# Gate and up products of both FFNs as seven half-size products instead of eight

## The chip, the cores and the metric

The kernel runs on one core of a Trainium2 chip. The metric is the device time of one execution in microseconds (us). Three runs of the kernel before gave a median of 1416.69 us (1415.98 to 1417.25). One further execution was taken by the hardware profiler.

The engines, by the names that the profile uses: PE is TensorE (matrix products, into PSUM), PEld its weight loads, DVE is VectorE, ACT is ScalarE, POOL is GpSimd, SP is SyncE, which here only issues DMAs (its queue is SPq). POOL issues DMAs too (POOLq).

## The reference

One layer for 512 tokens of width 1024 (`T = 512`, `D = 1024`, `FF = 2816`), all in float32:

```python
def swiglu(x, w_gate, w_up, w_down):
    return (jax.nn.silu(x @ w_gate) * (x @ w_up)) @ w_down

f = swiglu(rmsnorm(x, ffn1_pre_g[l]), ffn1_w_gate[l], ffn1_w_up[l], ffn1_w_down[l])
x = x + 0.5 * rmsnorm(f, ffn1_post_g[l])
y = hybrid_mixer(rmsnorm(x, mix_pre_g[l]), ...)   # windowed attention and mLSTM, merged
x = x + rmsnorm(y, mix_post_g[l])
f = swiglu(rmsnorm(x, ffn2_pre_g[l]), ffn2_w_gate[l], ffn2_w_up[l], ffn2_w_down[l])
x = x + 0.5 * rmsnorm(f, ffn2_post_g[l])
```

The change concerns `x @ w_gate` and `x @ w_up` in the two calls of `swiglu`. The mixer between them stays as it is.

## The kernel before, in words

Every float32 matrix product is made of three products of a rounded type (float32r): each operand is split into a high part and a low part, `ACT` casts the high part and `DVE` subtracts it from the original to get the low part, and PE accumulates high x high, high x low and low x high in one PSUM bank. `load_w` does this for a weight tile of 128 x 1024: SP issues a DMA into a buffer `wf` (three of them), ACT writes `wh`, DVE writes `wl` (five buffers each). The function `ws` then issues the products: for 8 blocks of 128 rows and 3 terms, 24 matmuls of 128x512.

The FFN (`ffn`) runs in two stages. In the first, the hidden width of 2816 is cut into `NF = 22` blocks of 128, the loop variable is `f`. For each block a gate tile and an up tile are loaded (`load_w`, L66 to L75), PE makes the two products (2 x 24 matmuls, L161) into two PSUM banks `pg`, ACT takes `silu` of the gate bank (tile `s`) and DVE multiplies it with the up bank into `aT[:, f, :]` (`close`, L224 and L225). The first two blocks (`EARLY = 2`) run interleaved in token halves (`by_halves`, L171, matmuls of 128x256), because the transposed input `hTh`/`hTl` (high and low part of the normalised tokens, [128, 8, 512] each) is still being finished. In the second stage (`down`) each `aT` block is split into `ah` and `al` (L246, L247), and PE accumulates 24 matmuls of 128x512 for each block into eight banks `acc` (L211 to L213). Names carry an `_a` for the first FFN and a `_b` for the second.

The program is written in Tile: the order of the instructions of each engine is set by a scheduler when the program is built, and buffers of one tag are handed on as their readers finish. Each engine works through its instructions strictly in that order, and one that waits holds up all that stand behind it. SP's queue in this stage holds nothing but weight loads; POOL's holds the vectors of gains, the small constants of the mixer and one `pow` for each normalisation.

Of the kernel before, what the change touches and what calls it, by code (L numbers as in the profile page):

```python
# [10 lines left out]
F32 = mybir.dt.float32  # L11
F32R = mybir.dt.float32r
# [4 lines left out]
P = 128  # L17
# [22 lines left out]
def tile_hybrid_block(ctx: ExitStack, tc: tile.TileContext, a: dict):  # L40
    nc = tc.nc

    const = ctx.enter_context(tc.tile_pool(name="const", bufs=1))
    wpool = ctx.enter_context(tc.tile_pool(name="wpool", bufs=1))
    act = ctx.enter_context(tc.tile_pool(name="act", bufs=1))
    small = ctx.enter_context(tc.tile_pool(name="small", bufs=4))
    psum = ctx.enter_context(tc.tile_pool(name="psum", bufs=8, space=bass.MemoryType.PSUM))
# [6 lines left out]

    warm = act.tile([P, 512], BF16, tag="tmp", bufs=1, name="warm")[:, 0:256]
# [4 lines left out]
    ident = const.tile([P, P], F32, name="ident")  # L60
    make_identity(nc, ident)
# [4 lines left out]
    def load_w(src, name, n=1024, after=()):  # L66
        wf = wpool.tile([P, WMAX], F32, tag="wf", bufs=3, name=f"wf_{name}")[:, :n]
        nc.sync.dma_start(wf, src)
        with ExitStack() as st:
            for i in after:  # L70
                st.enter_context(tc.issue_after(i))
            wh = wpool.tile([P, WMAX], F32R, tag="wh", bufs=5, name=f"wh_{name}")[:, :n]
            nc.scalar.copy(wh, wf)  # L73
            wl = wpool.tile([P, WMAX], F32R, tag="wl", bufs=5, name=f"wl_{name}")[:, :n]
            nc.vector.tensor_tensor(wl, wf, wh.bitcast(F32), op=ALU.subtract)  # L75
        return wh, wl

    def gain(src, name, eng=None):
        g = act.tile([P, D], F32, tag="gain", bufs=2, name=f"g_{name}")
        (eng or nc.gpsimd).dma_start(g, src.partition_broadcast(P))  # L80
        return g

    def rsqrt(v, n, name):
        r = small.tile([P, n], F32, tag="r", name=f"r_{name}")
        nc.gpsimd.tensor_tensor(r, v, nhalf[:, :n], op=ALU.pow)
        return r
# [90 lines left out]
    def new_hT(name):  # L177
        hTh = act.tile([P, KD, T], F32R, tag="hTh", name=f"hTh_{name}")
        hTl = act.tile([P, KD, T], F32R, tag="hTl", name=f"hTl_{name}")
        return hTh, hTl  # L180
# [36 lines left out]

    def ffn(pool, todo, first_w, hT, wgu, wd, post, finish, name, later=None, pins=()):
        hTh, hTl = hT
        aT = pool.tile([P, NF, T], F32, name=f"aT_{name}")  # L220

        def close(f, pg):
            s = pool.tile([P, T], F32, tag="s", bufs=2, name=f"s_{name}{f}")
            nc.scalar.activation(s, pg[0], AF.Silu)  # L224
            nc.vector.tensor_tensor(aT[:, f, :], pg[1], s, op=ALU.mult)  # L225
        early = []
        for f in range(EARLY):
            wg, wu = first_w if first_w and f == 0 else [load_w(wgu[f, b], f"{name}gu{f}{b}", after=pins if f + b else ()) for b in range(2)]
            early.append((wg, wu, pair(f"pg_{name}{f}")))
        by_halves([(pg, (wg, wu)) for wg, wu, pg in early], hTh, hTl, todo)  # L230
        for f in range(EARLY):
            close(f, early[f][2])
        if later:
            later()
        for f in range(EARLY, NF):
            wg = load_w(wgu[f, 0], f"{name}g{f}")
            wu = load_w(wgu[f, 1], f"{name}u{f}")
            pg = pair(f"pg_{name}{f}")
            ws(pg[0], wg, KD, hTh, hTl)
            ws(pg[1], wu, KD, hTh, hTl)  # L240
            close(f, pg)

        def get_x(kk):
            ah = pool.tile([P, T], F32R, tag="ah", bufs=5, name=f"ah_{name}{kk}")
            al = pool.tile([P, T], F32R, tag="al", bufs=5, name=f"al_{name}{kk}")
            nc.scalar.copy(ah, aT[:, kk, :])  # L246
            nc.vector.tensor_tensor(al, aT[:, kk, :], ah.bitcast(F32), op=ALU.subtract)  # L247
            return ah, al

        return down(pool, NF, lambda kk: wd[kk], get_x, post, finish, todo, name)  # L250


    with tc.tile_pool(name="ffn_a", bufs=1) as fa:
        hbuf = [(act, "h"), (fa, "h2")]
        tbuf = [(act, "tmp"), (fa, "tmp2")]
        def load_x(t):
# [10 lines left out]
        first_w = [load_w(a["wgu1"][0, b], f"agu0{b}", after=pins if b else ()) for b in range(2)]  # L267
        todo = []
# [21 lines left out]

        pins = ffn(fa, todo, first_w, hT1, a["wgu1"], a["wd1"], post1, finish1, "a", load_gains)
    hTh, hTl = hT


    mctx = ExitStack()
    mix = mctx.enter_context(tc.tile_pool(name="mix", bufs=1))
    atth = mix.tile([P, HEADS, T], F32R, name="atth")
    attl = mix.tile([P, HEADS, T], F32R, name="attl")
    cw = mix.tile([P, 16, 5], F32, name="cw")
    nc.gpsimd.dma_start(cw, a["convwb"])  # L300

# [3 lines left out]
    ropeS = ap_.tile([32, 1, T], F32, name="ropeS")  # L305
    nc.gpsimd.dma_start(ropeC, a["ropeC"])
    nc.gpsimd.dma_start(ropeS, a["ropeS"])
    masks = ap_.tile([P, 512], BF16, name="masks")
    nc.gpsimd.dma_start(masks, a["masks"])
# [4 lines left out]
    nc.gpsimd.dma_start(gb, a["gbias"])  # L314
    SWAP = [(i + 16) % 32 for i in range(32)]

    def qk_evac(h, g, pq):
        q = ap_.tile([P, 2, T], F32, tag="qk", bufs=4, name=f"qk_{h}{g}")
        for b in range(2):
            nc.scalar.copy(q[:, b, :], pq[b])  # L320
        for b in range(2):
            sw = act.tile([32, T], F32, tag="h", bufs=1, name=f"sw_{h}{g}{b}")
# [180 lines left out]

    ga = act.tile([4, 2, T], F32, tag="tmp", bufs=1, name="ga")
    gb4 = act.tile([4, 2, T], F32, tag="h", bufs=1, name="gb4")
    gc4 = act.tile([4, 2, T], F32, tag="gain", bufs=2, name="gc4")
# [3 lines left out]
    selr = act.tile([4, D], F32R, tag="gain", bufs=2, name="selr")  # L510
    Gh = selr[:, 512:1024]
# [32 lines left out]
    caus = mix.tile([P, 1, P], F32, name="caus")  # L544
    nc.gpsimd.dma_start(caus[:, 0, :], a["caus"])
    hg = act.tile([P, 1, D], F32, tag="gain", bufs=2, name="hg")
    nc.gpsimd.dma_start(hg[:, 0, :], a["mlstm_head_g"].partition_broadcast(P))
# [221 lines left out]

    g_post2 = gain(a["ffn2_post_g"], "f2post")  # L770
    with tc.tile_pool(name="ffn_b", bufs=1) as fb:
        def post3(t):
            return PostNorm(t, g_post2, [(act, "tmp"), (fb, "tmp2")][t % 2], "f2", True)
# [5 lines left out]
        ffn(fb, todo, None, hT2, a["wgu2"], a["wd2"], post3, finish3, "b", pins=pins)  # L779

# [30 lines left out]
def _layout(inp):  # L811
# [57 lines left out]
```

## Time and profile before

| | us |
|---|---|
| median of three runs | 1416.69 |
| the profiled execution | 1415.97 |
| its span in the trace | 1414.2 |
| PE busy (share of the span) | 1401.5 (99%) |
| DVE busy | 624.5 (44%) |
| ACT busy | 487.8 (34%) |
| first FFN, blocks 2 to 21 of gate and up, on the chain that ended last | 217.63 |
| second FFN, the same blocks | 217.63 |
| granted TensorE clock, mean | 0.999 |

A busy PE means that matmuls followed one another without a gap. Their ends are modelled and overlap the next one's start, so the pace is read from the distance of starts or from the length of a stretch divided by its count, not from the mean duration of one.

### The profile page before, as it was taken

What the parts mean: (1) busy time and instruction counts of PE and PEld (TensorE: products, weight loads), DVE (VectorE), ACT (ScalarE), POOL (GpSimd) and SP (SyncE); (2) the same over time, 40 slices, a digit from 0 to 9 for tenths busy, and PEclk for the clock granted to TensorE, in tenths of its full rate; (3) what the DMA queues carried; (4) which work ended last, traced back from release to release, by engine and by line L of the source; (5) the groups of instructions that cost most, each with busy time, mean ns of one, the idle gap of its engine ahead of it and who ended that gap; (6) DMA issues with size and microseconds to landing.
All of it is one profiled execution on the core that took longest, in us unless ns stands there. A gap on an engine that the chain in (4) does not pass through costs nothing.

```text
span 1414.2 us, 16603 instructions
## 1 busy us (share of the span) xinstructions
PE 1401.5 (99%) x6752; PEld 1185.0 (84%) x6752; DVE 624.5 (44%) x986; ACT 487.8 (34%) x761; POOL 29.1 (2%) x52
## 2 busy tenths in 40 slices
PE   8999999999999999999999999999999999999998
PEld 8888888888899889888888888888888888888886
DVE  5332222233772775565756743333374222222333
ACT  5322222232533632344544543222264222222222
POOL 1000000000110000000000000000010000000000
PEclk9999999999999999999999999999999999999999
DMA  6433333333143222222222232323323323333321
GB/s 238 119 92 102 96 98 95 99 90 92 50 123 110 86 75 75 77 73 75 83 82 77 86 106 75 104 90 92 102 75 119 103 92 96 98 102 92 90 75 60
DMA packets 37357, 133.12 MB, mean 94 GB/s; under 512 B 4268, under 2 KB 4268, under 8 KB 37280
## 3 DMA queue, kind: packets, MB, share of 16 engines
q1 hardware_dynamic: 36144, 128.50, 29.2%
q0 software_dynamic: 1136, 3.56, 0.9%
q8 instruction: 53, 0.87, 0.3%
q14 instruction: 24, 0.20, 0.0%
HBM read 129.95 MB, written 2.10 MB: 93 GB/s over the span
## 4 chain that ended last, share of the span: by engine, by line
PE 95%; DVE 2%; ACT 1%; issue 1%; DMA 0%; POOL 0%; SPq 0%; POOLq 0%; DVEq 0%; ACTq 0%
PE pg_b L161 15%; PE pg_a L161 15%; PE p L161 11%; PE pq L161 7%; PE pm L161 6%; PE acc_b L211 3%; PE acc_b L212 3%; PE acc_b L213 3%; PE acc_a L213 3%; PE acc_a L211 2%; PE acc_a L212 2%; PE pvo L591 2%; PE pvo L593 2%; PE pvo L592 2%; PE pg_a L171 2%; PE pg_b L171 2%
## 5 line engine op out<-in xcount | busy, mean ns | idle before, releaser
L211 PE MATMUL acc_a<-wh_ad,ah_a 128*128 128x512 f32 x176 | 69.5, 395 | 0.0
L211 PE MATMUL acc_b<-wh_bd,ah_b 128*128 128x512 f32 x176 | 69.4, 395 | 0.0
L213 PE MATMUL acc_b<-wl_bd,ah_b 128*128 128x512 f32 x176 | 69.4, 395 | 0.0
L212 PE MATMUL acc_b<-wh_bd,al_b 128*128 128x512 f32 x176 | 69.4, 395 | 0.0
L212 PE MATMUL acc_a<-wh_ad,al_a 128*128 128x512 f32 x176 | 69.4, 395 | 0.0
L213 PE MATMUL acc_a<-wl_ad,ah_a 128*128 128x512 f32 x176 | 69.4, 395 | 0.0
L161 PE MATMUL pq<-hTh_mx,wh_qk 128*128 128x512 f32 x160 | 63.5, 397 | 0.0
L161 PE MATMUL pq<-hTl_mx,wh_qk 128*128 128x512 f32 x160 | 62.4, 390 | 0.0
L161 PE MATMUL pg_b<-hTl_f,wh_bg 128*128 128x512 f32 x160 | 62.3, 389 | 0.0
L161 PE MATMUL pg_a<-hTl_f,wh_ag 128*128 128x512 f32 x160 | 62.3, 389 | 0.0
L161 PE MATMUL pg_a<-hTh_f,wh_ag 128*128 128x512 f32 x160 | 62.3, 389 | 0.0
L161 PE MATMUL pg_b<-hTh_f,wh_bg 128*128 128x512 f32 x160 | 62.3, 389 | 0.0
L161 PE MATMUL pg_a<-hTh_f,wh_au 128*128 128x512 f32 x160 | 62.2, 389 | 0.0
L161 PE MATMUL pg_a<-hTl_f,wh_au 128*128 128x512 f32 x160 | 62.2, 389 | 0.0
L161 PE MATMUL pg_b<-hTh_f,wh_bu 128*128 128x512 f32 x160 | 62.2, 389 | 0.0
L161 PE MATMUL pg_b<-hTl_f,wh_bu 128*128 128x512 f32 x160 | 62.2, 389 | 0.0
L75 DVE TENSOR_TENSOR wl_bd<-wf_bd,wh_bd 128x1024 fp32r<-128x1024 f32 x22 | 26.9, 1224 | 71.7 <-ACT wh_bd L73 71.7
L75 DVE TENSOR_TENSOR wl_ad<-wf_ad,wh_ad 128x1024 fp32r<-128x1024 f32 x22 | 26.9, 1224 | 71.8 <-ACT wh_ad L73 71.8
L75 DVE TENSOR_TENSOR wl_bu<-wf_bu,wh_bu 128x1024 fp32r<-128x1024 f32 x20 | 24.5, 1225 | 70.0 <-ACT wh_bu L73 62.3
L75 DVE TENSOR_TENSOR wl_au<-wf_au,wh_au 128x1024 fp32r<-128x1024 f32 x20 | 24.5, 1225 | 69.3 <-ACT wh_au L73 63.7
L73 ACT CAST wh_bd<-wf_bd 128x1024 fp32r<-128x1024 f32 x22 | 23.1, 1051 | 88.1 <-PE acc_b L212 70.2
L73 ACT CAST wh_ad<-wf_ad 128x1024 fp32r<-128x1024 f32 x22 | 23.1, 1051 | 88.0 <-PE acc_a L212 70.2
(339 smaller groups left out, 3419.4 us busy)
## 6 DMA issues: line engine op xcount, KB each, us to landing
wf_qk<-in_wqk SPq DMA_DIRECT2D x24, 512.0 KB, 3.6
wf_ad<-in_wd SPq DMA_DIRECT2D x22, 512.0 KB, 3.5
wf_bd<-in_wd SPq DMA_DIRECT2D x22, 512.0 KB, 3.5
wf_ag<-in_wgu SPq DMA_DIRECT2D x20, 512.0 KB, 3.6
wf_au<-in_wgu SPq DMA_DIRECT2D x20, 512.0 KB, 3.6
wf_bg<-in_wgu SPq DMA_DIRECT2D x20, 512.0 KB, 3.5
wf_bu<-in_wgu SPq DMA_DIRECT2D x20, 512.0 KB, 3.6
wf_mqk<-in_wmqk SPq DMA_DIRECT2D x16, 512.0 KB, 3.6
```

Source lines behind the costliest of these rows:

```text
L73: nc.scalar.copy(wh, wf)
L75: nc.vector.tensor_tensor(wl, wf, wh.bitcast(F32), op=ALU.subtract)
L161: nc.tensor.matmul(out, lhsT=wt[:, k * P:(k + 1) * P], rhs=x[:, k, tok], start=n == 0, stop=n == len(terms) - 1)
L171: nc.tensor.matmul(outs[b][:, tok], lhsT=ws_[b][w][:, k * P:(k + 1) * P], rhs=x[:, k, tok], start=i + k + hf == 0, stop=hf == 1 and i == 2 ...
L211: nc.tensor.matmul(out, lhsT=xh[:, tk], rhs=wh[:, cs], start=first, stop=False)
L212: nc.tensor.matmul(out, lhsT=xl[:, tk], rhs=wh[:, cs], start=False, stop=False)
L213: nc.tensor.matmul(out, lhsT=xh[:, tk], rhs=wl[:, cs], start=False, stop=last)
L591: nc.tensor.matmul(out, lhsT=hTh[:, k, tk], rhs=wh[:, cs], start=k == 0, stop=False)
L592: nc.tensor.matmul(out, lhsT=hTl[:, k, tk], rhs=wh[:, cs], start=False, stop=False)
L593: nc.tensor.matmul(out, lhsT=hTh[:, k, tk], rhs=wl[:, cs], start=False, stop=k == KD - 1)
```

## The change

For blocks `f` = 4 to 21 of both FFNs (`PLAIN = 4`; 18 blocks each), gate and up are no longer two products of [128 x 1024] by [1024 x 512]. They are written as one 2x2 block product: the contraction of 1024 is cut into two halves of 512, the tokens into two halves of 256, and gate and up are the two rows. Eight half-size products (128 x 512 by 512 x 256) are replaced by seven, each with 12 matmuls of 128x256 (L307), by a scheme of the Strassen kind. It needs sums of weight quarters, sums of input quarters and sums of results.

- Weights (`load_quads`): a block holds four quarters of 128 x 512, `q0` to `q3`. SP loads `f1` (q0 and q1), `f4` (q3) and `ab` (q2, twice); then POOL issues a DMA that adds q0 and q3 from memory onto the two halves of `ab` (`accum_op`, it waits until the load of `ab` has landed). DVE adds `f4` to the first half of `ab` into `cd[:, 0]` (L261) and `f1[:, 1]` to that into `cd[:, 1]` (L262). `f1`, `cd`, `ab` and `f4` are each split by ACT (L238) and DVE (L239) into the high and low parts for products 1 and 2, 6 and 3, 7 and 5, and 4. In the names below the number of the block and of the first product run together: `wl_a107` is block 10, product 7.
- Inputs (`token_parts`): four sums of input quarters, once for each FFN, made while blocks 2 and 3 run. The unused end of `aT` is the scratch.
- Results (`seven`): ACT copies product 1 out of PSUM (`q1`), DVE adds it to what the bank `qb` holds (`uv`, L331), and after further products makes `z` (L338, L339, L313); `silu` is taken in two halves, and DVE multiplies (L314). Product 4 of a block is issued inside the next block (`finish`).
- Memory: pools now stand on two sides of SBUF, scratch tiles that lived in `act` move to a pool `work` that is opened for each phase; `wf` moves to `act`. The loads of the gains for the post norms move from the first blocks to the start of `down` (`begin`). The mixer's small constants are issued behind the last `pow` of the first FFN (`mixer_from`).
- The host lays out gate and up of a block side by side ([22, 128, 2048] instead of [22, 2, 128, 1024]).

```diff
+    def load_quads(src, low, scr, name):
+        q = src.rearrange("p (q c) -> p q c", c=Q)
+        f1 = act.tile([P, 2, Q], F32, tag="wf", bufs=3, name=f"f1_{name}")
+        f4 = scr.tile([P, Q], F32, tag="wf4", bufs=2, name=f"f4_{name}")
+        ab = act.tile([P, 2, Q], F32, tag="wf", bufs=3, name=f"ab_{name}")
+        nc.sync.dma_start(ab, q[:, 2:3, :].broadcast_to([P, 2, Q]))
+        nc.sync.dma_start(f1, q[:, 0:2, :])
+        nc.sync.dma_start(f4, q[:, 3, :])
+        nc.gpsimd.dma_start(ab, q[:, 0:4:3, :], accum_op=ADD)
...
+        pair_of((1, 2), f1)
+        cd = scr.tile([P, 2, Q], F32, tag="cd", bufs=1, name=f"cd_{name}")
+        nc.vector.tensor_tensor(cd[:, 0, :], ab[:, 0, :], f4, op=ADD)
+        nc.vector.tensor_tensor(cd[:, 1, :], cd[:, 0, :], f1[:, 1, :], op=ADD)
+        pair_of((6, 3), cd)
+        pair_of((7, 5), ab)
...
+    def token_parts(low, tmp, hTh, hTl, name):
...
+        nc.vector.tensor_tensor(f[5], b11, b12, op=SUB)
+        nc.vector.scalar_tensor_tensor(f[6], f[5], -1.0, b22, op0=MUL, op1=SUB)
+        part(6)
+        part(5)
+        nc.vector.tensor_tensor(f[7], b22, b12, op=SUB)
+        part(7)
+        nc.vector.scalar_tensor_tensor(f[4], f[6], -1.0, b21, op0=MUL, op1=SUB)
+        part(4)
...
+    def seven(fs, wgu, x, low, scr, aT, name):
...
+        for f in fs:
...
+            product(a1, w[1], 1, True, False)
+            nc.scalar.copy(q1, a1)
+            product(b1, w[6], 6, True, False)
+            product(c1, w[5], 5, False, False)
+            nc.vector.tensor_tensor(uv, bc, q1[:, None, :].broadcast_to([P, 2, H]), op=ADD)
+            if prev:
+                finish(prev)
+            product(a1, w[2], 2, False, True)
+            nc.scalar.activation(s[:, 0, :], a1, AF.Silu)
+            product(b1, w[7], 7, False, False)
+            product(c1, w[3], 3, False, True)
+            nc.vector.tensor_tensor(z[:, 1, :], b1, uv[:, 1, :], op=ADD)
+            nc.vector.tensor_tensor(z[:, 2, :], c1, uv[:, 0, :], op=ADD)
+            nc.scalar.activation(s[:, 1, :], z[:, 2, :], AF.Silu)
...
-        for f in range(EARLY, NF):
-            wg = load_w(wgu[f, 0], f"{name}g{f}")
-            wu = load_w(wgu[f, 1], f"{name}u{f}")
-            pg = pair(f"pg_{name}{f}")
-            ws(pg[0], wg, KD, hTh, hTl)
-            ws(pg[1], wu, KD, hTh, hTl)
-            close(f, pg)
+            for f in range(EARLY, PLAIN):
...
+                    x = token_parts(low, aT[:, NF - 16:, :], hTh, hTl, name)
...
+            seven(range(PLAIN, NF), wgu, x, low, scr, aT, name)
```

What the scheduler makes of it is seen on DVE and on SP in the middle of the first FFN's gate and up stage. DVE before, for two blocks (`wl` is the low part of a gate tile `ag` or an up tile `au`, `aT_a` the product that closes a block):

```order
L75 TENSOR_TENSOR wl_ag9_901<-wf_ag9_897,wh_ag9_899 128x1024
L75 TENSOR_TENSOR wl_au9_907<-wf_au9_903,wh_au9_905 128x1024
L225 TENSOR_TENSOR aT_a_195<-pg_a7_1_780,s_a7_829 128x512
L75 TENSOR_TENSOR wl_ag10_966<-wf_ag10_962,wh_ag10_964 128x1024
L75 TENSOR_TENSOR wl_au10_972<-wf_au10_968,wh_au10_970 128x1024
L225 TENSOR_TENSOR aT_a_195<-pg_a8_1_845,s_a8_894 128x512
```

DVE in the changed kernel, for one block's worth of work (from one `cd` to the next there are these eleven; block 11's weights, block 10's `uv`, block 9's results):

```order
L261 TENSOR_TENSOR cd_a11_1473<-ab_a11_1464,f4_a11_1463 128x512
L239 TENSOR_TENSOR wl_a107_1357<-ab_a10_1340,wh_a107_1356 128x1024
L262 TENSOR_TENSOR cd_a11_1473<-cd_a11_1473,f1_a11_1462 128x512
L239 TENSOR_TENSOR wl_a111_1470<-f1_a11_1462,wh_a111_1469 128x1024
L338 TENSOR_TENSOR z_a9_1244<-qb_a9_1241,uv_a9_1243 128x256
L339 TENSOR_TENSOR z_a9_1244<-qb_a9_1241,uv_a9_1243 128x256
L239 TENSOR_TENSOR wl_a116_1477<-cd_a11_1473,wh_a116_1476 128x1024
L331 TENSOR_TENSOR uv_a10_1367<-qb_a10_1365,q1_a10_1366 128x512
L313 TENSOR_TENSOR z_a9_1244<-qb_a9_1241,q1_a9_1242 128x256
L239 TENSOR_TENSOR wl4_a11_1485<-f4_a11_1463,wh4_a11_1484 128x512
L314 SCALAR_TENSOR_TENSOR aT_a_205<-z_a9_1244,s_a9_1245 128x512
```

Three instructions of a block have become eleven, and the first of them, the sum of block 11 that needs the accumulated `ab_a11`, stands ahead of the split of block 10's `ab`.

SP's weight loads before, for three blocks:

```order
L68 DMA wf_ag9_897<-in_wgu1 128x1024
L68 DMA wf_au9_903<-in_wgu1 128x1024
L68 DMA wf_ag10_962<-in_wgu1 128x1024
L68 DMA wf_au10_968<-in_wgu1 128x1024
L68 DMA wf_ag11_1027<-in_wgu1 128x1024
L68 DMA wf_au11_1033<-in_wgu1 128x1024
```

SP's weight loads in the changed kernel, for two blocks (`ab` is the load of the doubled quarter onto which POOL's DMA then adds):

```order
L248 DMA f4_a11_1463<-in_wgu1 128x512
L246 DMA ab_a11_1464<-in_wgu1 128x2x512
L247 DMA f1_a11_1462<-in_wgu1 128x1024
L248 DMA f4_a12_1587<-in_wgu1 128x512
L246 DMA ab_a12_1588<-in_wgu1 128x2x512
L247 DMA f1_a12_1586<-in_wgu1 128x1024
```

Two loads of a block have become three, with a fourth on POOL's queue. In the built program the `f1` of every block lies in the same one of the three buffers of tag `wf`, and `ab` alternates between the other two, so the load of `ab_a12` overwrites `ab_a10` and waits for the last reader of it, `wl_a107`.

More of the change, by code (lines that the diff above doesn't have):

```diff
@@ L78, in gain @@
     def gain(src, name, eng=None):
-        g = act.tile([P, D], F32, tag="gain", bufs=2, name=f"g_{name}")
+        g = work.tile([P, D], F32, tag="gain", bufs=2, name=f"g_{name}")
         (eng or nc.gpsimd).dma_start(g, src.partition_broadcast(P))
         return g
+    last_pow = [None]
     def rsqrt(v, n, name):
         r = small.tile([P, n], F32, tag="r", name=f"r_{name}")
-        nc.gpsimd.tensor_tensor(r, v, nhalf[:, :n], op=ALU.pow)
+        last_pow[0] = nc.gpsimd.tensor_tensor(r, v, nhalf[:, :n], op=ALU.pow).ins
         return r
@@ L219, in ffn @@
+    PLAIN = 4
+    def ffn(pool, todo, first_w, hT, wgu, wd, post, finish, name, begin=None, pins=()):
         hTh, hTl = hT
         aT = pool.tile([P, NF, T], F32, name=f"aT_{name}")
[L222 to L229, printed above, removed]
@@ L248, in get_x @@
             return ah, al
[L250 to L255, printed above, removed]
+        pins = down(pool, NF, lambda kk: wd[kk], get_x, post, finish, todo, name)
+        dn.close()
+        return pins
+    with new_pool("ffn_a") as fa:
+        hbuf = [(work, "h"), (work, "h2")]
+        tbuf = [(work, "tmp"), (work, "tmp2")]
+        op_ctx = ExitStack()
+        work.pool = op_ctx.enter_context(new_pool("opening"))
         def load_x(t):
@@ L266, in tile_hybrid_block @@
             turned = pins[0]
-        first_w = [load_w(a["wgu1"][0, b], f"agu0{b}", after=pins if b else ()) for b in range(2)]
+        first_w = [load_w(a["wgu1"][0, :, b * 1024:(b + 1) * 1024], f"agu0{b}", after=pins if b else ()) for b in range(2)]
         todo = []
@@ L305, in tile_hybrid_block @@
     ropeS = ap_.tile([32, 1, T], F32, name="ropeS")
[L306 removed]
+    with tc.issue_after(mixer_from):
+        nc.gpsimd.dma_start(ropeC, a["ropeC"])
     nc.gpsimd.dma_start(ropeS, a["ropeS"])
     masks = ap_.tile([P, 512], BF16, name="masks")
[L309 removed]
+    with tc.issue_after(mixer_from):
+        nc.gpsimd.dma_start(masks, a["masks"])
     perm = ap_.tile([P, 72], F32, name="perm")
@@ L313, in tile_hybrid_block @@
     gb = mix.tile([4, 2], F32, name="gb")
-    nc.gpsimd.dma_start(gb, a["gbias"])
+    with tc.issue_after(mixer_from):
+        nc.gpsimd.dma_start(gb, a["gbias"])
     SWAP = [(i + 16) % 32 for i in range(32)]
@@ L509, in tile_hybrid_block @@
     ones4, Gm = gc4[:, 0, :], gc4[:, 1, :]
-    selr = act.tile([4, D], F32R, tag="gain", bufs=2, name="selr")
+    selr = work.tile([4, D], F32R, tag="gain", bufs=2, name="selr")
     Gh = selr[:, 512:1024]
@@ L544, in tile_hybrid_block @@
     caus = mix.tile([P, 1, P], F32, name="caus")
-    nc.gpsimd.dma_start(caus[:, 0, :], a["caus"])
-    hg = act.tile([P, 1, D], F32, tag="gain", bufs=2, name="hg")
+    with tc.issue_after(mixer_from):
+        nc.gpsimd.dma_start(caus[:, 0, :], a["caus"])
+    hg = work.tile([P, 1, D], F32, tag="gain", bufs=2, name="hg")
     nc.gpsimd.dma_start(hg[:, 0, :], a["mlstm_head_g"].partition_broadcast(P))
@@ L767, in tile_hybrid_block @@
     mctx.close()
-    g_post2 = gain(a["ffn2_post_g"], "f2post")
-    with tc.tile_pool(name="ffn_b", bufs=1) as fb:
+    g_post2 = []
+    with new_pool("ffn_b") as fb:
         def post3(t):
-            return PostNorm(t, g_post2, [(act, "tmp"), (fb, "tmp2")][t % 2], "f2", True)
+            return PostNorm(t, g_post2[0], [(work, "tmp"), (work, "tmp2")][t % 2], "f2", True)
         def finish3(t):
```

160 lines of the change are left out of this document (128 added, 32 removed).

## The prediction

> **What bounds the kernel now.** I read the page's busy shares and slices first, then the chain that ended last, then the stretch of gate and up, then single durations.
>
> ```profile
> span 1414.2 us, 16603 instructions
> PE 1401.5 (99%) x6752; PEld 1185.0 (84%) x6752; DVE 624.5 (44%) x986; ACT 487.8 (34%) x761; POOL 29.1 (2%) x52
> PEclk9999999999999999999999999999999999999999
> DMA  6433333333143222222222232323323323333321
> PE 95%; DVE 2%; ACT 1%; issue 1%; DMA 0%; POOL 0%; SPq 0%; POOLq 0%; DVEq 0%; ACTq 0%
> ```
>
> PE has work 99% of the span at full clock, and the chain is PE for 95% of it. No other engine and no transfer sets the time; only less work on PE, or a new wait, can change it. The chain in order of time (start, length, what) gives PE's pace:
>
> ```profile
> 21.90 15.35 PE pg_a L171 x128
> 37.24 217.63 PE pg_a L161 x960
> ...
> 1067.48 217.63 PE pg_b L161 x960
> ```
>
> 128 matmuls of 256 columns take 15.35 us, 0.120 each; 960 of 512 columns take 217.63 us, 0.2267 each. A block of gate and up (48 matmuls) is 217.63 / 20 = 10.88 us. The same stretch by windows (PE, PEld, DVE, ACT, POOL busy, then clock, DMA share, GB/s):
>
> ```profile
> 37.20:254.90 217.70, 217.70 (x962) 180.31 (x961) 63.68 (x65) 56.67 (x64) 0.00 (x0) 1.00 0.33 100
> ```
>
> DVE is busy 29% here, ACT 26%, the DMA engines 33%. There is room beside PE, and the change fills it.
>
> **PE's part.** A changed block has 7 x 12 = 84 matmuls of 256 columns: 84 x 0.120 = 10.07 us for 10.88. That is 0.81 us, or 7.4%, not the eighth that seven for eight promises, because a matmul of half the width takes 53% of the time. The wider rows of the list of groups say the same if read rightly: their mean is a latency (283 ns against 389), and the starts are what count.
>
> ```profile
> L171 PEld LDWEIGHTS pg_a<-hTh_f,wh_agu x64: 186/192/192, 11.9 to 33.0; 128*128 128x128 f32 x64
> ```
>
> A weight load shows 192 ns, which would make 16.1 us of 84; but in that stretch a load went with every matmul and the pace was 0.120, so the loads overlap. If nothing else waits, 2 FFNs x 18 blocks x 0.81 = 29 us go.
>
> **DVE and ACT.** Durations by shape:
>
> ```profile
> L75 DVE TENSOR_TENSOR wl_ag<-wf_ag,wh_ag 128x1024 fp32r<-128x1024 f32 x20 | 24.3, 1215 | 0.0
> L225 DVE TENSOR_TENSOR aT_a<-pg_a,s_a 128x512 f32<-128x512 f32 x22 | 15.2, 691 | 85.3 <-PE pg_a L161 84.6 <-ACT s_a L224 0.8
> L601 DVE TENSOR_TENSOR vml<-pvo,vmh 128x256 fp32r<-128x256 f32 x16 | 6.7, 420 | 0.0
> L73 ACT CAST wh_ag<-wf_ag 128x1024 fp32r<-128x1024 f32 x20 | 21.1, 1054 | 50.9 <-PE pg_a L161 50.9
> L246 ACT CAST ah_a<-aT_a 128x512 fp32r<-128x512 f32 x22 | 13.6, 618 | 6.5 <-DVE aT_a L225 6.5
> L603 ACT ACTIVATE so<-pvo 128x256 f32<-128x256 f32 x16 | 6.2, 385 | 12.5 <-DVE vml L601 12.5
> L247 DVE TENSOR_TENSOR al_a<-aT_a,ah_a 128x512 fp32r<-128x512 f32 x22 | 15.1, 684 | 0.0
> ```
>
> DVE's eleven instructions of a block: three splits of 1024 columns (3 x 1.22), five of 512 columns (two sums `cd`, the split `wl4`, `uv`, the closing product, 5 x 0.69) and three `z` of 256 (3 x 0.42): 8.4 us. ACT: 3 x 1.05 + 0.62 + three of 256 columns at 0.385 = 4.9 us. Both are below 10.07, so neither is the bound by its sum, but DVE is full enough that the order of its instructions matters. `token_parts` is four sums, four combinations and four splits of 1024 columns, 12 x 1.22 = 14.6 us of DVE once for each FFN, beside blocks 2 and 3 (21.8 us of PE), where DVE has only 2 x 3.1 us of its own: it just fits. SP issues three loads instead of two, POOL one more; POOL has nothing else there. All of these lie beside PE and I cost them at nothing; if `token_parts` overran, it would cost its overrun once.
>
> **The ring, on which the forecast rests.** In the changed order DVE's sum `cd_a11` waits for the accumulating DMA of block 11, and queued behind it on DVE are `wl_a107` (PE's products 5 and 7 of block 10 need it), the first split of block 11 and the `z` of block 9 (product 4 of block 9 needs its first). So PE runs at most about one block ahead of the accumulates. And the accumulates feed themselves: `ab_a12` may be loaded only after `wl_a107` has read `ab_a10`; `wl_a107` stands behind `cd_a11`; `cd_a11` waits for accumulate 11; accumulate 12 waits for the load of `ab_a12`. One turn of this ring is one block:
>
> accumulate lands -> `cd` -> `wl` -> load of `ab` -> accumulate lands.
>
> Two rows of DVE's timeline give the first two links (starts 0.61 apart, then 1.22):
>
> ```profile
> 102.66 0.69 DVE L225 TENSOR_TENSOR aT_a<-pg_a,s_a 128x512 f32<-128x512 f32 x1 [4.23 <-PE pg_a L161]
> 103.27 1.22 DVE L75 TENSOR_TENSOR wl_ag<-wf_ag,wh_ag 128x1024 fp32r<-128x1024 f32 x1
> ```
>
> The transfers (KB, median us from issue to landing):
>
> ```profile
> wf_ag<-in_wgu SPq DMA_DIRECT2D x20, 512.0 KB, 3.6
> wf_v<-in_wv SPq DMA_DIRECT2D x2, 260.0 KB, 2.9
> g_mpre<-in_mix_pre_g POOLq DMA_DIRECT2D x1, 512.0 KB, 5.2
> hg<-in_mlstm_head_g POOLq DMA_DIRECT2D x1, 512.0 KB, 4.3
> g_f2post<-in_ffn_post_g POOLq DMA_DIRECT2D x1, 512.0 KB, 4.5
> cw<-in_convwb POOLq DMA_DIRECT2D x1, 40.0 KB, 3.6
> ```
>
> The load of `ab` is 512 KB on SP's queue: 3.6. The turn is 0.61 + 1.22 + 3.6 + A, with some 0.1 between the queues: 5.5 + A, where A is the accumulating DMA from issue to landing. The trace has no such DMA. Lower bound: it costs no more than the quickest plain one of its size on POOL's queue, `hg`, 4.3. Upper bound: every byte is fetched twice and written once, one after the other. 252 KB more took 0.7 us on SP's queue (2.9 to 3.6), so 512 KB more take 1.4; two more passes on 4.5 make 7.3. I take one more pass, since the old contents of `ab` must be read besides the two quarters: A = 4.5 + 1.4 = 5.9, from `g_f2post`, which ran beside least. The turn is then 11.4 us, above PE's 10.07 and above the 10.88 of before.
>
> The Trainium skill's page "Collectives: The Full Stack" (The bandwidth ceiling: the fold count and why AG ≠ RS ≠ AR) says that a reduce in the DMA engines runs at half a copy's rate, because it reads two sources on one ring. By it one more pass is the right price and the sum stays what it is; no row of this trace shows a reduce.
>
> **The sum for one FFN.** Before: 18 x 10.88 = 195.8. After: the first three blocks have their weights ready from blocks 2 and 3 and run at PE's pace, 3 x 10.07 = 30.2; fifteen run at the ring's, 15 x 11.4 = 171.0; at the switch to `down` the memory of the input sums is reused, and `ah` and `al` of the first block (0.62 + 0.68), hidden before, stand open, with the closing of the last block about 2. Together 203.2, so +7.4, twice +15. On the profiled execution's 1415.97 (1414.2 of it span) that is 1431; the median of the runs is 0.7 above that execution, which makes 1432. The ring costs 30 us of time for each us of A; no change would be at a turn of (195.8 - 32.2) / 15 = 10.9, A = 5.4.
>
> Other edits:
>
> ```profile
> 6.49 0.71 POOL L80 DMA_DIRECT2D g_f1post<-in_ffn_post_g  x1
> 19.52 0.58 POOL L80 DMA_DIRECT2D g_mpre<-in_mix_pre_g  x1 [2.56 <-DVE h_f L125]
> 361.99 0.56 POOL L85 TENSOR_TENSOR r_pf<-v_pf,nhalf 128x1 f32<-128x1 f32 x1 [341.88 <-DVE v_pf L96]
> ```
>
> The gains move from 6.5 and 19.5 us to the start of `down` at 255, 100 us before the norm that uses them at 362; the constants of the mixer issue where they did, behind the last `pow`; the sides of SBUF change addresses alone; weight slices keep runs of 4 KB. I cost these at nothing: what covers them is the rest of `down`, and a transfer 5 us late would still be early.
>
> **Rivals.**
>
> 1. *The accumulate is as quick as a copy, and PE stays the bound (faster).* With A up to 4.5 the turn is at most 10.0, under PE's 10.07. Then 18 x 10.07 + 2 = 183.3 for each FFN, -12.5, twice -25: 1391. For it: the DMA engines are idle two thirds of this stage, and `cw` shows that 3.6 of a POOL transfer is there at 40 KB. Against: a plain copy already took 4.3 to 5.2, and this one moves more in shorter runs of 2 KB. The point from which it decides is A = 5.4; between 4.5 and 5.4 the gain shrinks from 25 to nothing.
>    The Trainium skill's page "DMA: Bandwidth & Descriptors" (Anatomy of one DMA — SWDGE (gpsimd) path) would have it so: 2.0 us plus bytes over 436 GB/s is an estimate of 3.2 for 512 KB and 4.4 with a second read. The plain ones of this trace took 4.3 to 5.2, so I trust it little.
> 2. *The accumulate moves its bytes in series.* A = 7.3, a turn of 12.8: 30.2 + 192 + 2 = 224.2, +28.4 for each FFN, 1473. For it: `g_mpre` at 5.2 shows that POOL's transfers stretch beside others, and the load of `f4` falls into the accumulate.
> 3. *The products don't run at half pace.* Were the 192 ns of the weight loads the pace, a block would take 16.1 us. The 15.35 us for 128 exclude it.
> 4. *DVE is the bound.* 8.4 of 10.07: only if sums or PSUM reads take 20% longer than the rows; I give it no time of its own.
>
> **How the numbers follow.** About 0.2% (3 us) is what can be told from no change here. My own case (A from 5.5 to 6.6, 1418 to 1452) has 0.40, rival 2 and beyond 0.20, rival 1 with its part gains 0.35, and 0.05 lies within 0.2%. Rivals 3 and 4 get nothing. So faster 0.35, same 0.05, slower 0.60. The predicted time is my case's, 1432, with a range of its own from 1418 to 1452. For 8 in 10 the range must take in the full gain and nearly all of rival 2: 1389 to 1470.
>
> **What would show it.** Right, if in blocks 6 to 21 the starts of a line's DVE rows are 11 us or more apart, DVE's idle time stands before `cd` (L261) with the DMA `ab<-in_wgu` as releaser, SP's load of `ab` waits for `wl` (L239), and PE's gaps lie before products 4 and 5. The row of POOL's `ab<-in_wgu` among the DMA issues tells A at once. Wrong, if that row is below 5.4: then the pace of L307 is 0.120 without gaps, blocks are 10.1 apart, and the end comes near 1391; or if PE's gaps follow DVE while the accumulates are long there.

## The result, and the profile after

| | us |
|---|---|
| changed kernel, median of 4 runs | 1528.57 (1525.80 to 1535.53) |
| kernel before, on the same chip, median of 4 runs | 1416.97 |
| ratio, 95% interval | 1.0796 (1.0760 to 1.0833) |
| span of the profiled execution (before 1414.2) | 1526.8 |

The change costs 112 us; the forecast was 15, with a range up to 1470. The page of the changed kernel (busy shares, clock slices, the chain by engine and by line):

```profile
PE 1424.8 (93%) x8048; PEld 1271.2 (83%) x8048; DVE 816.6 (53%) x1298; ACT 566.8 (37%) x913; POOL 73.4 (5%) x88
...
PEclk9999888899999999999999999999999789899999
...
PE 68%; DMA 17%; DVE 9%; issue 4%; ACT 1%; POOL 0%; DVEq 0%; SPq 0%; POOLq 0%; ACTq 0%
PE p L176 10%; DMA ab_b<-in_wgu 9%; DMA ab_a<-in_wgu 7%; PE pq L176 7%; PE pm L176 6%; PE qb_b L307 3%; PE qb_a L307 3%; PE acc_b L227 3%; PE acc_b L228 3%; PE acc_b L226 3%; PE acc_a L227 2%; PE acc_a L228 2%; PE acc_a L226 2%; PE pvo L747 2%; PE pvo L749 2%
```

PE was 95% of the chain and is 68%. What took its place is the DMA into `ab`, with 16%. The groups of instructions say who waits for it (busy and mean ns, then the idle time of the engine just before, and its releaser):

```profile
L261 DVE TENSOR_TENSOR cd_b<-ab_b,f_b 128x512 f32<-128x512 f32 x18 | 12.5, 693 | 105.8 <-DMA ab_b<-in_wgu 99.5
...
L261 DVE TENSOR_TENSOR cd_a<-ab_a,f_a 128x512 f32<-128x512 f32 x18 | 12.5, 692 | 100.0 <-DMA ab_a<-in_wgu 97.0
```

DVE stands idle some 200 us in front of 36 sums `cd`, as the prediction said it would where the ring decides. The DMA issues give the two prices (KB each, median us from issue to landing):

```profile
ab_a<-in_wgu SPq DMA_DIRECT2D x18, 512.0 KB, 5.4
ab_a<-in_wgu POOLq DMA_DIRECT2D x18, 512.0 KB, 6.9
...
ab_b<-in_wgu SPq DMA_DIRECT2D x18, 512.0 KB, 5.5
ab_b<-in_wgu POOLq DMA_DIRECT2D x18, 512.0 KB, 7.0
```

The accumulate takes 6.9 to 7.0 (forecast 5.9), and the load of `ab` 5.4 to 5.5 (forecast 3.6). One turn of the ring in the first FFN, from the timelines of DVE, SP and POOL (start, length; SP and POOL issue DMAs here):

```profile
171.46 0.69 DVE L261 TENSOR_TENSOR cd_a<-ab_a,f_a 128x512 f32<-128x512 f32 x1 [6.62 <-DMA ab_a<-in_wgu]
172.06 1.22 DVE L239 TENSOR_TENSOR wl_a<-ab_a,wh_a 128x1024 fp32r<-128x1024 f32 x1
```

```profile
157.82 0.38 SPq L246 DMA_DIRECT2D ab_a<-in_wgu  x1
...
173.31 0.38 SPq L246 DMA_DIRECT2D ab_a<-in_wgu  x1
```

```profile
163.88 1.20 POOL L249 DMA_DIRECT2D ab_a<-in_wgu  x1 [12.55 <-DVE z_a L313]
```

SP issues the load at 157.82, POOL the accumulate 6.06 later, `cd` starts 7.58 after that, and SP issues the next load 1.85 after `cd`: 15.5 us. This load landed after 5.5 us, so about 0.6 lies between the queues; this accumulate landed after 7.6, above the median. (The releaser that the row names for POOL, `z_a`, only ended near that time. In the turn before, where POOL's row names the load itself, the issue also stands 0.56 behind the landing, 150.12 after 149.56.) Over a whole stage the turn is read from the first and last start of `cd` (the row gives min, median and max ns, then those starts):

```profile
L261 DVE TENSOR_TENSOR cd_a<-ab_a,f_a x18: 685/693/694, 45.4 to 289.3; 128x512 f32<-128x512 f32 x18
L261 DVE TENSOR_TENSOR cd_b<-ab_b,f_b x18: 691/693/694, 1126.4 to 1376.9; 128x512 f32<-128x512 f32 x18
```

17 distances in 243.9 and 250.5 us: 14.3 and 14.7 each, the quick first ones included.

### The profile page after: what moved, and what is told of

The parts are those of the page before. It is cut to its first block, busy times and chain, and to the rows that moved or that the text cites. A ratio compares the mean times of both kernels' runs of the same rounds, so it can differ in the third digit from the quotient of the medians.

```text
span 1526.8 us, 19969 instructions
## 1 busy us (share of the span) xinstructions
PE 1424.8 (93%) x8048; PEld 1271.2 (83%) x8048; DVE 816.6 (53%) x1298; ACT 566.8 (37%) x913; POOL 73.4 (5%) x88
## 4 chain that ended last, share of the span: by engine, by line
PE 68%; DMA 17%; DVE 9%; issue 4%; ACT 1%; POOL 0%; DVEq 0%; SPq 0%; POOLq 0%; ACTq 0%
PE p L176 10%; DMA ab_b<-in_wgu 9%; DMA ab_a<-in_wgu 7%; PE pq L176 7%; PE pm L176 6%; PE qb_b L307 3%; PE qb_a L307 3%; PE acc_b L227 3%; PE acc_b L228 3%; PE acc_b L226 3%; PE acc_a L227 2%; PE acc_a L228 2%; PE acc_a L226 2%; PE pvo L747 2%; PE pvo L749 2%
## 5 line engine op out<-in xcount | busy, mean ns | idle before, releaser
L261 DVE TENSOR_TENSOR cd_b<-ab_b,f_b 128x512 f32<-128x512 f32 x18 | 12.5, 693 | 105.8 <-DMA ab_b<-in_wgu 99.5
L261 DVE TENSOR_TENSOR cd_a<-ab_a,f_a 128x512 f32<-128x512 f32 x18 | 12.5, 692 | 100.0 <-DMA ab_a<-in_wgu 97.0
L238 ACT CAST wh_b<-cd_b 128x1024 fp32r<-128x1024 f32 x18 | 18.8, 1046 | 98.0 <-DVE cd_b L262 89.7
L88 DVE TENSOR_TENSOR wl_qk<-wf_qk,wh_qk 128x1024 fp32r<-128x1024 f32 x24 | 29.3, 1221 | 47.4 <-ACT wh_qk L86 33.9
L238 ACT CAST wh_a<-cd_a 128x1024 fp32r<-128x1024 f32 x18 | 18.8, 1046 | 93.4 <-DVE cd_a L262 91.9
L176 PE MATMUL pm<-hTh_mx,wh_mqk 128*128 128x512 f32 x128 | 50.4, 394 | 0.0
L747 PE MATMUL pvo<-wh_vo,hTh_mx 128*128 128x512 f32 x128 | 50.2, 392 | 0.0
L176 PE MATMUL pm<-hTl_mx,wh_mqk 128*128 128x512 f32 x128 | 49.9, 390 | 0.0
L176 PE MATMUL p<-hTh_mx,wh_gm 128*128 128x512 f32 x128 | 49.9, 390 | 0.0
L749 PE MATMUL pvo<-wl_vo,hTh_mx 128*128 128x512 f32 x128 | 49.8, 389 | 0.0
```

The source lines that it names most:

```text
L176: nc.tensor.matmul(out, lhsT=wt[:, k * P:(k + 1) * P], rhs=x[:, k, tok], start=n == 0, stop=n == len(terms) - 1)
L238: nc.scalar.copy(wh, src)
L261: nc.vector.tensor_tensor(cd[:, 0, :], ab[:, 0, :], f4, op=ADD)
L747: nc.tensor.matmul(out, lhsT=hTh[:, k, tk], rhs=wh[:, cs], start=k == 0, stop=False)
L749: nc.tensor.matmul(out, lhsT=hTh[:, k, tk], rhs=wl[:, cs], start=False, stop=k == KD - 1)
```

## The experiments

**1. Order alone.** The first `cd` of a block is queued behind the split of the block before's `ab`, so that split no longer waits for an accumulate. Every instruction and transfer stays; the scheduler also moved the second sum of `cd` (now L267), behind the first split and two `z`.

```diff
+            if keys[0] == 7:
+                last_split[0] = lo_ins
...
-        nc.vector.tensor_tensor(cd[:, 0, :], ab[:, 0, :], f4, op=ADD)
+        with tc.issue_after(last_split[0]) if last_split[0] else nullcontext():
+            nc.vector.tensor_tensor(cd[:, 0, :], ab[:, 0, :], f4, op=ADD)
```

> Every transfer and every sum stays; one thing is moved: on DVE the sum cd of a block is queued behind the split of the previous block's ab (wl_a107 ahead of cd_a11) instead of ahead of it. Theory 1 (the ring: accumulate lands, cd 0.61, wl 1.22, load of ab 5.9 to POOL's issue, accumulate 7.0, which makes the 14.9 us per block of the changed kernel): the load of ab for a block no longer stands behind the accumulate before it, two of these chains overlap, and a block falls from 14.9 to 10.1 to 11.6 us; time 1395 to 1425. Rival A (throughput: the queues and DMA engines cannot deliver a block's 1.75 MB faster than once in about 15 us): nothing changes, 1515 to 1535. Rival B (PE at a granted clock of 0.88 in this stage, or its 256-column products, set the pace): nothing changes either.

Measured: 1408.35 us (1405.91 to 1412.94), 0.9952 of before (0.9932 to 0.9971). 120 us go with the new order on DVE, though the accumulates take longer in the first FFN (6.9 before) and little less in the second (7.0 before):

```profile
ab_a<-in_wgu POOLq DMA_DIRECT2D x18, 512.0 KB, 7.8
...
ab_b<-in_wgu POOLq DMA_DIRECT2D x18, 512.0 KB, 6.7
```

From 60 to 240 us the DMA engines now move 165 GB/s (126 in the changed kernel, 60 to 310 us), and the same products run at a granted clock of 1.00 (0.88 there). So rivals A and B fall: neither the throughput of the DMA engines nor the clock that PE is granted for these products made the time; the order in DVE's queue, which closed the ring, did. In the rows below the split of `ab` ends at 154.36, SP issues the next load of `ab` at 154.39, and only then does DVE stand 2.33 us in front of `cd`:

```profile
153.14 1.22 DVE L239 TENSOR_TENSOR wl_a<-ab_a,wh_a 128x1024 fp32r<-128x1024 f32 x1
156.70 0.69 DVE L266 TENSOR_TENSOR cd_a<-ab_a,f_a 128x512 f32<-128x512 f32 x1 [2.33 <-DMA ab_a<-in_wgu]
```

**2. No adding.** POOL's DMA copies instead of adding.

```diff
-        nc.gpsimd.dma_start(ab, q[:, 0:4:3, :], accum_op=ADD)
+        nc.gpsimd.dma_start(ab, q[:, 0:4:3, :])
```

> POOL's DMA writes the two quarters into ab without adding them (the weight sums are left out, so products 3, 5, 6 and 7 have other weights); size, runs, queue, waits and order are the same. Theory 1: the turn of the ring is 7.9 us plus the landing of this DMA. If adding costs one more pass over 512 KB, the copy lands at about 5.6 and the time falls by 30 us for each us, to about 1485; if the adding is most of it (landing 4.5), 1450. Rival D (POOL's issue with runs of 2 KB is what takes the time, not the adding): landing stays near 7, time 1520 to 1535.

Measured: 1449.44 us (one run), 79 us less.

```profile
ab_a<-in_wgu SPq DMA_DIRECT2D x18, 512.0 KB, 5.2
ab_a<-in_wgu POOLq DMA_DIRECT2D x18, 512.0 KB, 4.6
```

In the same place of the program the copy takes 4.6 where the accumulate takes 6.9: adding costs 2.3 us of latency (second FFN: 4.4 and 7.0, so 2.6). That is the case in which the adding is most of it (1450). Even free of it the kernel is 33 us slower than before, so adding is not the whole cause; the load of `ab` is still 5.2.

**3. No accumulate at all.** SP loads the four quarters in two transfers with runs of 4 KB, and DVE makes the two sums as well, into a tile `ab` of their own.

```diff
...
-        nc.sync.dma_start(ab, q[:, 2:3, :].broadcast_to([P, 2, Q]))
         nc.sync.dma_start(f1, q[:, 0:2, :])
-        nc.sync.dma_start(f4, q[:, 3, :])
-        nc.gpsimd.dma_start(ab, q[:, 0:4:3, :], accum_op=ADD)
+        nc.sync.dma_start(f3, q[:, 2:4, :])
+        f4 = f3[:, 1, :]
...
+        nc.vector.tensor_tensor(ab[:, 0, :], f3[:, 0, :], f1[:, 0, :], op=ADD)
+        nc.vector.tensor_tensor(ab[:, 1, :], f3[:, 0, :], f3[:, 1, :], op=ADD)
```

> The seven products stay; POOL's accumulating DMA and the doubled load of ab are gone. SP loads the four quarters in two transfers of 512 KB, and DVE makes all four weight sums (two more adds of 128x512 per block). Theory 1 (transfers in the ring are the loss): PE sets the pace again, 10.1 us per block, about 1392 (1388 to 1400). Rival C (DVE: its instructions of a block come to 9.8 us by duration, so it is the bound): 1400 to 1425. Rival B (clock or products on PE): above 1450, with the clock below 0.95 in the stage.

Measured: 1384.28 us (1383.85 to 1384.49), 0.9771 of before (0.9757 to 0.9786): the fastest of all versions, and 4 us below the expected range, which counted nothing for the layout (experiment 4). A window of the first FFN's gate and up stage (PE, PEld, DVE, ACT, POOL busy; clock, DMA share, GB/s):

```profile
60.00:240.00 180.00, 180.00 (x1501) 179.85 (x1499) 154.08 (x221) 83.30 (x123) 0.00 (x0) 1.00 0.30 102
```

DVE is busy 86% of this stretch and PE has no gap, so rivals B and C fall. Two sums of 0.69 more for each block, some 25 us of DVE in each FFN, cost nothing that shows.

**4. The layout alone.** All 22 blocks plain; the pools on two sides, the gains and constants stay as changed.

```diff
-    PLAIN = 4
+    PLAIN = NF
```

> Only the rest of the change: two-sided SBUF, the pools, the moved gains and constants, gate and up side by side in memory, but all 22 blocks as plain products. Theory 1: the rest costs nothing, 1417 within 3. Rival E (part of the loss comes from the new layout and its waits): over 1420.

Measured: 1407.20 us (1406.81 to 1408.17), 0.9934 (0.9920 to 0.9949). Both expectations missed: the part that I costed at nothing gains 9.7 us. Most of it is found where no product of the change runs. The matmuls of `down` (`acc`; busy time, then mean ns), first in the kernel before, then here:

```profile
L211 PE MATMUL acc_a<-wh_ad,ah_a 128*128 128x512 f32 x176 | 69.5, 395 | 0.0
```

```profile
L226 PE MATMUL acc_a<-wh_ad,ah_a 128*128 128x512 f32 x176 | 68.6, 389 | 0.0
```

**5. One run instead of the same quarter twice.** The load of `ab` fetches two neighbouring quarters, in runs of 4 KB.

```diff
-        nc.sync.dma_start(ab, q[:, 2:3, :].broadcast_to([P, 2, Q]))
+        nc.sync.dma_start(ab, q[:, 2:4, :])
```

> Changed kernel, but the load of ab fetches q2 and q3 as one run of 4 KB for each partition instead of q2 twice in runs of 2 KB (so two of the seven weight sums are other sums; everything waits as before). Theory R (the doubled quarter in 2 KB runs makes the load of ab slow): ab on SP's queue falls from 5.4 us to about 3.8, the accumulate on POOL's queue stays near 6.9, a turn of the ring falls from 15.0 to 13.4 us, and the time falls by 30 blocks x 1.6 = 48 us to about 1480. Rival S (the load is slow because f1 and f4 are issued right behind it and share the DMA engines): ab stays at 5.2 or more and the time stays within 10 us of 1528.

Measured: 1471.33 us (1469.53 to 1474.43), ratio 1.0392 (1.0374 to 1.0411); 57 us less than the changed kernel (48 expected).

```profile
ab_a<-in_wgu SPq DMA_DIRECT2D x18, 512.0 KB, 3.5
ab_a<-in_wgu POOLq DMA_DIRECT2D x18, 512.0 KB, 6.8
```

The load falls by 1.9 us with `f1` and `f4` still behind it, so rival S falls.

**6. Matmuls and DMAs by themselves.**

> Not the layer: two measurements alone, with nothing beside them, and an output that is not the reference's. Part 1: ten groups of 192 matmuls of 128x512 like those of down, with the token operand (128 columns at a time) and the weight operand (512 columns) at chosen SBUF addresses: as in the kernel before (BF: 191 KB + 800 B and 44 KB + 672 B), as in the changed one (LL: 88 KB + 640 B and 16 KB + 640 B), and with height and remainder exchanged. Theory H (height): the groups whose token operand lies at 191 KB or 188 KB (HL, BF, HB, OB, HH) have a pace near 0.2325 us, the low ones (LL, LB) 0.2267, whatever the remainder. Theory M (remainder): the groups whose two operands leave different remainders (BF, LB, OB, OM) are the slow ones, HL and HB are fast. Theory C (company): all ten are at 0.2267, and it was what ACT, DVE and the DMAs did beside them. Part 2: seven kinds of DMAs of 512 KB, each alone, six times. Theory R: the doubled quarter (bc) takes 1 us or more longer than one run of 4 KB (run); rival S: both take 3.6 us alone. The accumulate (ac) alone takes 5.5 to 7 us if adding is dear in itself, near the plain copy on the same queue (cp, about 4.4) if it was the company of the other loads.

The DMAs, each alone, 512 KB:

```profile
bc<-in_wgu SPq DMA_DIRECT2D x6, 512.0 KB, 4.5
run<-in_wgu SPq DMA_DIRECT2D x6, 512.0 KB, 3.5
two<-in_wgu SPq DMA_DIRECT2D x6, 512.0 KB, 3.6
cp<-in_wgu POOLq DMA_DIRECT2D x6, 512.0 KB, 4.0
...
ac<-in_wgu POOLq DMA_DIRECT2D x6, 512.0 KB, 5.8
```

Theory R needs a correction: two different quarters in runs of 2 KB (`two`) take no longer than one run (`run`). It is reading the same quarter twice (`bc`) that costs 1.0 us alone; in the kernel, where experiment 5 changed the length of the runs with it, the difference is 1.9. The accumulate (`ac`) takes 5.8 alone, 1.8 more than the copy (`cp`); the other 1.1 of the kernel's 6.9 come where other transfers run beside it (a copy: 4.0 alone, 4.6 in experiment 2). Which of them it is was not tried.

The matmul groups (start, length, and the group's name after `acc`):

```profile
99.88 44.96 PE L82 MATMUL accBF<-big 128*128 128x512 f32 x192
144.68 44.96 PE L82 MATMUL accLB<-big 128*128 128x512 f32 x192
189.48 43.73 PE L82 MATMUL accHB<-big 128*128 128x512 f32 x192
233.05 44.96 PE L82 MATMUL accOB<-big 128*128 128x512 f32 x192
277.85 43.71 PE L82 MATMUL accOL<-big 128*128 128x512 f32 x192
321.39 43.68 PE L82 MATMUL accOM<-big 128*128 128x512 f32 x192
```

The starts of BF, LB and OB stand 44.8 us ahead of the next one, 0.2333 for each matmul; those of HB, OL and OM 43.5, 0.2268. Height is not it (HB lies as high as BF and is fast, LB as low as LL and is slow), nor is company, since nothing else ran. Theory M holds if the remainder is that by 256, which it had not said: it had OM among the slow, but OM's operands, at 896 and 640 B behind a full KB, both leave 128. BF and LB leave 32 and 160, OB 128 and 160.

**7. The remainder in the kernel before, and its period.**

```diff
+        nc.vector.memset(pool.tile([P, 32], F32, name=f"pad_{name}"), 0.0)
         aT = pool.tile([P, NF, T], F32, name=f"aT_{name}")
```

> The kernel before, with 128 unused bytes at the front of the pool of each FFN: ah and al then begin at addresses that leave 160 when divided by 256, as wh and wl do (they left 32). Nothing else changes. Theory M (remainder): the pace of down falls from 0.2325 to 0.2267 us for each of 2 x 528 matmuls, down gets 2.6 to 3.1 us shorter in each FFN, the time falls by 5 to 6.5 us to about 1411. Rival (it is what else the two-sided layout changed): no change, within 1 us.

> The same with 256 unused bytes: every address of these pools moves, the remainders by 256 stay. Theory M: no change, 1416.5 to 1417.3 us. Rival (any shift of these tiles does it): 5 us or more faster.

> Not the layer: groups of 192 matmuls alone as in down, one after the other; the first (WU) warms up. Weight operand at 44 KB + 160 B, token operand at 96 KB + 160 B + d, with d = 32, 64, ... 224 B in groups A to G. Groups H, I, J: weight operand at 44 KB, token operand at 96 KB + 0, 128 and 256 B. Theory M with 256 B as the period: H and J (difference 0 and 256) at 389 ns and a length of 43.6 us, all others at 395 ns and 44.8. If the period is 64 B or 128 B, B, D and F (64) or D and I (128) are fast too; the earlier groups with differences of 128 and 224 B, which were slow, speak against it.

Measured: 1411.51 us with 128 bytes (0.9963, 0.9951 to 0.9976), 1417.02 with 256 (0.9999, 0.9991 to 1.0008). The row of the first FFN's `down` in the version with 128 bytes (min, median, max ns, first and last start), then with 256:

```profile
L211 PE MATMUL acc_a<-wh_ad,ah_a x176: 389/389/476, 255.3 to 375.2; 128*128 128x512 f32 x176
```

```profile
L211 PE MATMUL acc_a<-wh_ad,ah_a x176: 390/393/477, 255.7 to 378.6; 128*128 128x512 f32 x176
```

From the first to the last start this row takes 119.9 us with 128 bytes and 122.9 with 256. 128 idle bytes give 5.45 us of time, and the same shift twice gives nothing. So the remainders of `down` are 5.5 of the 9.7 us. The mixer's merge and its output product are 1.8 and 1.2 us shorter in experiment 4, with means of 389 to 392 ns for their matmuls there and 391 to 399 before; that their remainders are the cause was not tried, and the last 1.2 us stay open. The single groups:

```profile
236.59 44.97 PE L83 MATMUL accE<-big 128*128 128x512 f32 x192
281.39 44.12 PE L83 MATMUL accF<-big 128*128 128x512 f32 x192
325.35 44.96 PE L83 MATMUL accG<-big 128*128 128x512 f32 x192
370.15 43.74 PE L83 MATMUL accH<-big 128*128 128x512 f32 x192
413.72 44.79 PE L83 MATMUL accI<-big 128*128 128x512 f32 x192
458.35 43.69 PE L83 MATMUL accJ<-big 128*128 128x512 f32 x192
```

H and J (equal remainders by 256) are fast and I (128 apart) is slow, as expected; A to E and G are slow. F, with a difference of 192, lies two thirds of the way from E to H, which the theory doesn't say: equal remainders are safe, but the rule for unequal ones stays open, and so does its mechanism.

**8. The two sums on GpSimd instead of DVE.** The lines are shown against experiment 3.

```diff
-        nc.vector.tensor_tensor(ab[:, 0, :], f3[:, 0, :], f1[:, 0, :], op=ADD)
-        nc.vector.tensor_tensor(ab[:, 1, :], f3[:, 0, :], f3[:, 1, :], op=ADD)
+        nc.gpsimd.tensor_tensor(ab[:, 0, :], f3[:, 0, :], f1[:, 0, :], op=ADD)
+        nc.gpsimd.tensor_tensor(ab[:, 1, :], f3[:, 0, :], f3[:, 1, :], op=ADD)
```

> As the variant with all weight sums on VectorE (1384.3 us), but the two sums that make ab run on GpSimd. If DVE's 63% were costing anything there, the time falls by up to 3 us; if the sums are slower on GpSimd and come late for products 7 and 5, it rises, by 20 us or more if they take over 4 us each; my own expectation is the same time within 3 us.

Measured: 1397.22 us (0.9859, 0.9844 to 0.9874), 13 us slower than experiment 3: a miss. DVE's own instructions got longer:

```profile
L239 DVE TENSOR_TENSOR wl_a<-f_a,wh_a 128x1024 fp32r<-128x1024 f32 x18 | 36.4, 2024 | 5.3 <-ACT wh_a L238 5.3
L262 DVE TENSOR_TENSOR cd_a<-ab_a,f_a 128x512 f32<-128x512 f32 x18 | 21.5, 1194 | 2.9 <-POOL ab_a L260 2.9
```

The same split takes 1.22 us and the same sum 0.69 in experiment 3. The Trainium skill's page "SBUF — State Buffer" (Who interferes with whom) says that a DVE instruction with two SBUF inputs contends with a GpSimd instruction that reads SBUF; these rows agree. The starts of `cd` stand 10.6 and 10.7 us apart in the two FFNs instead of 10.3, which over their 34 distances is 12 of the 13 us; which link of a block makes them longer I did not trace.

## Why the prediction was wrong, by its own steps

The direction and the mechanism held: a ring of accumulate, `cd`, `wl`, load and accumulate sets the pace, DVE idles before `cd`, and PE's gaps lie before products 4 and 5 (rows at the end of this document). The sizes of the ring's links did not hold.

| step of the prediction | forecast | measured | what showed it |
|---|---|---|---|
| `cd` and `wl` up to the issue of the load | 0.61 + 1.22 | 1.85 | timelines |
| load of `ab` | 3.6 | 5.4 to 5.5 | DMA issues; 3.5 in experiment 5 |
| between the queues | 0.1 | about 0.6 (6.06 less the 5.5 of that load) | timelines |
| accumulate A | 5.9 | 6.9 to 7.0 | DMA issues; 5.8 alone |
| turn, mean over 17 distances | 11.2 (2 x 10.07, 15 x 11.4) | 14.3 and 14.7 | starts of `cd` |
| sides of SBUF and the other edits | 0 | -9.7 us, 5.45 of it by addresses in `down` | experiments 4 and 7 |

**The load of `ab` is the step that failed most.** "The load of `ab` is 512 KB on SP's queue: 3.6" took the row of a load that reads every byte once, at the same size and on the same queue; but the diff says `broadcast_to`. That row had no bound around it, though the operation was as foreign to the trace of before as the accumulate. 1.8 us too little, times 30, are 54 us. With 1.0 for A and 0.5 for the hand-over the turn of 11.4 becomes 14.7. These 3.3 us, times 30, are 99 of the 106 us by which the ring cost more than forecast (1529 against 1432, and the 9.7 that the other edits gave back).

**A was mis-sized in its pass.** The sum took 4.5 for a copy and 1.4 for one more pass. The copy takes 4.6 and 4.4 in the kernel (experiment 2), so the 4.5 held; the adding puts 2.3 to 2.6 on top of it. That makes A 1.0 us too short, 30 us of time. Alone the adding costs 1.8 and the accumulate 5.8; that this lies next to the forecast of 5.9 is luck, because a lone copy takes 4.0 and not 4.5. Rival 2's price of 7.3 came nearer, and the company of other transfers was among its reasons; how many passes the adding makes no run shows. Rival 1 falls: even a copy in its place leaves the ring at 12.2 us against PE's 10.07, and the lone accumulate, 5.8, stands above the 5.4 from which it decides. By the Trainium skill's page "DMA: Bandwidth & Descriptors" (Anatomy of one DMA — SWDGE (gpsimd) path) an estimate for 512 KB is 3.2 us for the copy and 4.4 with the bytes counted twice for the accumulate; alone they took 4.0 and 5.8.

**The rule of 30 us per us nearly holds.** Experiment 5 took 1.9 to 2.0 us off the load and 57 off the time. Where the time went, the starts of `cd` show in every version: 2 x 17 distances, with those of experiment 3 (10.3) as the base, and the products worked out from the starts before rounding:

| version | mean distance | 34 x (distance - 10.3) | time over experiment 3 |
|---|---|---|---|
| changed kernel | 14.5 | 144 | 144.3 |
| 5, one run | 12.8 | 86 | 87.1 |
| 2, copy | 12.2 | 66 | 65.2 |
| 1, order | 11.1 | 26 | 24.1 |

The rows behind it, of experiments 5, 2, 1 and 3 in this order (first FFN; the second is within 0.2 us of each):

```profile
L261 DVE TENSOR_TENSOR cd_a<-ab_a,f_a x18: 689/693/694, 45.8 to 263.8; 128x512 f32<-128x512 f32 x18
```

```profile
L261 DVE TENSOR_TENSOR cd_a<-ab_a,f_a x18: 686/693/694, 45.4 to 252.8; 128x512 f32<-128x512 f32 x18
```

```profile
L266 DVE TENSOR_TENSOR cd_a<-ab_a,f_a x18: 684/693/694, 45.0 to 234.6; 128x512 f32<-128x512 f32 x18
```

```profile
L262 DVE TENSOR_TENSOR cd_a<-ab_a,f_a x18: 684/686/689, 47.5 to 221.9; 128x512 f32<-128x512 f32 x18
```

**PE's part was right.** Experiment 3 is 22.9 us faster than experiment 4, which has the same layout and plain products; rival 1 priced the products at 25 for a ring that doesn't bind. The 2 us at the switch to `down` are there too, as gaps of 1.15 and 0.53 us of PE in experiment 3. **DVE is not the bound** held too: with 9.8 us of work for each block it kept up. **"The sides of SBUF change addresses alone"** stood in the prediction, and I costed addresses at nothing without a row for it. The rows were there: the same 128x512 matmuls stood at 389 ns in gate and up and at 395 in `down`, and I read past them.

Put together: 1416.9 before, 9.7 off for the layout, 22.9 off for the products, 144.3 on for the ring (the changed kernel against experiment 3) make 1528.6.

## What to carry to other kernels

When a transfer feeds a buffer that the same transfer must wait for, add up the whole turn and price every link by its own access pattern and its own company, the plain ones too. A sum on an engine with idle time beside the bound (36 x 2 sums of 0.69 us on DVE) can be cheaper than one that rides free on a DMA, because the DMA's latency stands in the turn and DVE's busy time does not: 1384 us against 1408 even with the better order. And where an instruction in an in-order queue waits for a transfer, what is queued behind it decides the price: the same work in another order was worth 120 us here.

## What the runs showed of the hardware

- A load that reads the same 256 KB twice took 4.5 us alone against 3.5 to 3.6 for 512 KB read once, and 5.4 against 3.5 beside other loads.
- An accumulating DMA of 512 KB took 5.8 us alone against 4.0 for the copy on the same queue; 6.9 against 4.6 in the kernel.
- A float32r matmul of 128x512 with equal remainders by 256 of its operands' addresses ran every 0.2268 us alone, with unequal ones every 0.2333 in most groups (0.2290 at a difference of 192 bytes); in the kernel before, 128 unused bytes were worth 5.45 us.
- After some short gaps PE starts its matmuls little more than half as often for a while. In the changed kernel:

```profile
156.35 0.28 PE L307 MATMUL qb_a<-x5l_a,wh_a 128*128 128x256 f32 x1
157.84 0.74 PE L307 MATMUL qb_a<-x5h_a,wl_a 128*128 128x256 f32 x4 [1.21 <-DVE wl_a L239]
160.25 0.58 PE L307 MATMUL qb_a<-x4h_a,wh_a 128*128 128x256 f32 x1 [1.66 <-DVE z_a L339]
160.63 0.42 PE L307 MATMUL qb_a<-x4l_a,wh_a 128*128 128x256 f32 x1
160.84 0.41 PE L307 MATMUL qb_a<-x4h_a,wh_a 128*128 128x256 f32 x1
```

After two gaps of 1.21 and 1.66 us the starts are 0.21 apart instead of 0.12, and the granted clock from 160 to 165 us is 0.50; from 166 us on they are 0.12 apart again. Such gaps did not always do it: gaps of 1.58 and 1.67 in the block at 131 us of the same trace were followed by starts 0.12 apart, and in experiment 2 a gap of 1.2 to 1.7 before product 4 was followed by 0.21 in two of the fourteen blocks from 96 to 257 us and by 0.12 in the others. The Trainium skill's page "TensorE: Matmul & The Clock Gate" (HAM oscillation — how this bites in real kernels) gives gaps above some 3.4 us as the ones to avoid; here the slow stretches came behind shorter ones, and what decides is open. Whether that pace cost anything by itself was not tried; in the turn shown DVE stood 6.6 us waiting for the transfer behind it, so there it was hidden.
